# Gate and up products as a seven-product 2x2 block scheme, two tile pairs per part in native float32

## The chip, the cores and the metric
One core of one Trainium2 chip. The metric is the device time of one execution in microseconds; lower is better. Everything is float32 in memory. The kernel is written in Python over the engines' instructions: TensorE (PE) multiplies into PSUM, VectorE (DVE), ScalarE (ACT) and GpSimd (POOL) work element by element, SyncE (SP) issues the transfers.

## The reference, cut to what matters
Two layers of a streaming encoder for 592 tokens (16 learned ones, 512 of a prompt, 64 of a sample stream) with 1024 features. Each layer:

```python
h = h + 0.5 * swiglu(rms(h), wa_gate, wa_up, wa_down)      # 1024 -> 2816 -> 1024
h = h + mixer(rms(h))                                       # Mamba-2 and HGRN2 heads side by side
h = h + 0.5 * swiglu(rms(h), wb_gate, wb_up, wb_down)
# swiglu(x) = (silu(x @ w_gate) * (x @ w_up)) @ w_down
```

and a last RMS norm. So there are four SwiGLU parts (ffa and ffb of two layers); each has 22 pairs of gate and up tiles of 128 columns and 8 tiles of 128 output features. The states of the mixers are outputs too; the change doesn't touch them.

## The kernel before
Features lie on partitions, tokens along the rows, in two halves of 296 (288 in the last part, which leaves the learned tokens out). A product with weights is exact to float32 by splitting both sides into two float32r parts, high and low, and adding three products: high x high, high x low, low x high (lines 476, 477, 478; x first in the profile's names). The weights are split on chip after loading: the high part by ScalarE (line 430), the low part, raw minus high, by VectorE (line 437), 1024 elements per partition in one instruction each. The parts of the normed x (`nh`, `nl`) are made by `Norm.parts` (lines 578 to 582) from the residual `h` and the norm's weights; the factor 1/rms is applied after the product, in the sinks (`gate` line 647, `up` line 658), so a product needn't wait for it. `Norm.finish` computes it (sums of squares on TensorE, a power on GpSimd, spread to all partitions by TensorE, written by ScalarE at line 538).

The work is a list of `Job`s in the order of the weights: for each chunk of feature tiles (8, 7 and 7) gate and up tile by tile, then the eight `down` jobs of the chunk, whose sinks add to `h` (line 686). `products` walks this list on TensorE; `fetch` loads the raw weights in the same order (512 KB a load, three raw buffers, two of each split part).

What each engine does next is decided before the run by a planner. Every task is a Python generator that yields (engine, estimated ns, what it waits for, buffers needed) before each step; `Plan.run` always issues the step that can start first, with the lower rank among equals. A step may name two engines; the one that would end first gets it:

```python
t = yield (V, G), (ns_dve(n), ns_pool(n)), (t,), () if k0 else (blo,)
(V, G)[plan.pick].tensor_tensor(job.lo[:, k0:k1], job.raw[:, k0:k1], job.hi[:, k0:k1].bitcast(F32),
                                op=ALU.subtract)
```

The planner's costs are `ns_dve(n) = 68 + n / 0.96`, `ns_act(n) = 100 + n / 1.2`, `ns_pool(n) = 40 + 2.26 n`; it knows nothing of engines disturbing each other. Each engine then runs its own list in order, held only by semaphores. PSUM has four buffers for products with weights (`mm`) and four for all else (`aux`); 32 buffers of 592 columns (`bT`) serve everything in between.

Of the kernel before, what the change touches and what calls it, by code (L numbers as in the profile page):

```python
# [16 lines left out]
P = 128  # L17
# [27 lines left out]
def constants():  # L45
    """Constants of the shapes alone."""
# [60 lines left out]

def ns_dve(n):
# [76 lines left out]
def body(ctx: ExitStack, tc: tile.TileContext, a: dict, o: dict):  # L185
# [41 lines left out]
    # parameters with features on partitions, [128, layers * tiles of 128 features] each  # L227
# [39 lines left out]
    def load_scalars():  # L267
        # per-head scalars: dt_bias on 8 partitions; -exp(a_log) on all; d_skip by feature
# [21 lines left out]
        # lower bounds of the forget gates: clip(cumsum(softmax) - softmax[0], 0, 1 - 1e-6)  # L290
# [16 lines left out]
        # log(max(lb, 1e-30)) in two parts, each within Ln's range  # L307
# [70 lines left out]
    class Job:  # L378
# [3 lines left out]
        def __init__(self, name, src, ks, x, ev, hvs, sink, rank=1, few=0):  # L382
            self.rank, self.few = rank, few
            self.name, self.src, self.ks, self.x, self.ev, self.hvs, self.sink = name, src, ks, x, ev, hvs, sink
            self.ready = [Ev() for _ in ks]
# [3 lines left out]
    def fetch():  # L389
# [4 lines left out]
        for b in range(3):  # L394
            yield from fetch_x(b, 0)
            if b == 0:
                load_columns("a", [("ffa", 16, lt(a["ln_ffa_w"]))], -1)
        for i, job in enumerate(jobs):
            nk = len(job.ks)
            src = job.src.rearrange("(k p) c -> p k c", p=P)  # L400
            first = i == 0
            for k0, k1 in ((0, 4), (4, 8)) if first else ((0, nk),):
                t = yield "DMA", 190 * (k1 - k0), (), () if k0 else (braw,)
                if k0 == 0:
                    job.raw = braw.tile(f"wr{i}")
                SP.dma_start(job.raw[:, k0:k1, :src.shape[2]], src[:, k0:k1])
                split = Ev()
                plan.add(-1 if i < 2 else 0, convert(i, job, k0, k1, t + 2000.0, prev, split))
                prev = split
                if first:  # L410
                    for b, g in ((0, 1), (1, 1), (2, 1)) if k0 == 0 else ():
                        yield from fetch_x(b, g)
# [8 lines left out]
    def convert(i, job, k0, k1, t, prev, split):  # L421
        if job.few:
            yield from convert_few(i, job, t, prev, split)
            return
        n = (k1 - k0) * P
        t = yield (S, G), (ns_act(n), 700 + 0.95 * n), (t, prev) if prev else (t,), () if k0 else (bhi,)
        if k0 == 0:
            job.hi = bhi.tile(f"wh{i}")
        if plan.pick == 0:
            S.activation(job.hi[:, k0:k1], job.raw[:, k0:k1], AF.Copy)  # L430
        else:
            G.tensor_scalar(job.hi[:, k0:k1], job.raw[:, k0:k1], 1.0, 0.0, op0=ALU.mult, op1=ALU.add)
        split.set(0.0)
        t = yield (V, G), (ns_dve(n), ns_pool(n)), (t,), () if k0 else (blo,)
        if k0 == 0:
            job.lo = blo.tile(f"wl{i}")
        (V, G)[plan.pick].tensor_tensor(job.lo[:, k0:k1], job.raw[:, k0:k1], job.hi[:, k0:k1].bitcast(F32),  # L437
                                        op=ALU.subtract)
        if k1 == len(job.ks):
            braw.put(t)  # L440
        for r in job.ready[k0:k1]:
            r.set(t)

    def convert_few(i, job, t, prev, split):
        n = job.few
        t = yield S, ns_act(40 * KD), (t, prev), (bhi,)
        job.hi = bhi.tile(f"wh{i}")
        S.activation(job.hi[:, :, 0:40], job.raw[:, :, 0:40], AF.Copy)
        split.set(0.0)
        t = yield V, ns_dve(n * KD), (t,), (blo,)  # L450
        V.tensor_tensor(job.hi[:, :, 32:32 + n], job.raw[:, :, 0:n], job.hi[:, :, 0:n].bitcast(F32), op=ALU.subtract)
        braw.put(t)
        for r in job.ready:
            r.set(t)

    def products():
        # the first two jobs and the last two take turns, a half of the tokens each
        steps = [(job, hv) for job in jobs[2:-2] for hv in job.hvs]
        steps = [(job, hv) for hv in jobs[0].hvs for job in jobs[:2]] + steps
# [1193 lines left out]
```

## Time and profile before

| | |
|---|---|
| median of 3 runs | 2437.81 us (2435.04 to 2440.62) |
| span of the profiled execution | 2435.3 us (no separate device time is recorded for it) |
| TensorE busy | 2410.6 us, 99% |
| VectorE, ScalarE, GpSimd busy | 1329.0, 815.1, 148.8 us |
| moved by DMA | 188.16 MB, mean 77 GB/s |

A profile line of a group reads: source line, engine, operation, output <- inputs (partitions x elements), count, busy us and mean ns of one. Matmuls overlap in their pipeline, so a matmul's own duration (about 0.30 us) is longer than the distance from one start to the next; the distance, or pitch, is what counts for time. A line of the timeline reads: start, duration (of all xN together), engine, line, operation; in square brackets the idle time before it and what ended that.

### The profile page before, as it was taken

To read this page: it belongs to the slowest core of one execution; us is meant where nothing else is said; L and a number is where in the kernel's file an instruction comes from. 1 tells how busy PE (TensorE), PEld (TensorE's weight loads), DVE (VectorE), ACT (ScalarE), POOL (GpSimd) and SP (SyncE) were. 2 spreads that over 40 slices of the span, in tenths; PEclk is the share of its full clock that TensorE was granted. 3 is DMA by queue.
4 is the path that set the end of the run, shared out by engine and by line. 5 is a ranking of instruction groups with operands and counts; after the bars stand their busy time and mean duration, and the time that the engine had idled before them with its cause. 6 is when DMAs were issued, how large, how long until landed. Compare 5 with 4: busy or idle time off the path is not lost.

```text
span 2435.3 us, 42176 instructions
## 1 busy us (share of the span) xinstructions
PE 2410.6 (99%) x17919; PEld 2382.4 (98%) x17919; DVE 1329.0 (55%) x2431; ACT 815.1 (33%) x1450; POOL 148.8 (6%) x202
## 2 busy tenths in 40 slices
PE   8999999999999999999999999999999999999999
PEld 8999999999899999999999999999998999999998
DVE  6434345579957543444554343455799675444344
ACT  5212223346344321222333122233464543222232
POOL 2000000011301000000000000000122110000002
PEclk9999999999999999999999999999999999999999
DMA  5222222331112322222222222223311132322322
GB/s 152 78 79 83 82 79 78 81 85 42 28 49 74 92 78 82 82 81 79 78 87 79 79 86 80 78 79 87 79 42 37 48 96 79 87 82 78 92 76 78
DMA packets 363979, 188.16 MB, mean 77 GB/s; under 512 B 10384, under 2 KB 361408, under 8 KB 363792
## 3 DMA queue, kind: packets, MB, share of 16 engines
q1 hardware_dynamic: 363792, 185.47, 26.8%
q8 instruction: 141, 2.31, 0.4%
q14 instruction: 46, 0.38, 0.0%
HBM read 180.94 MB, written 4.51 MB: 76 GB/s over the span
## 4 chain that ended last, share of the span: by engine, by line
PE 95%; DVE 3%; POOL 1%; ACT 0%; issue 0%; DMA 0%; SPq 0%; DVEq 0%; ACTq 0%; POOLq 0%
PE pd L476 8%; PE pd L477 8%; PE pd L478 8%; PE pu L476 8%; PE pu L478 8%; PE pg L476 8%; PE pu L477 8%; PE pg L478 8%; PE pg L477 8%; PE px L478 1%; PE px L476 1%; PE px L477 1%; PE po L476 1%; PE po L478 1%; PE po L477 1%; PE pa L1024 1%
## 5 line engine op out<-in xcount | busy, mean ns | idle before, releaser
L430 ACT ACTIVATE wh<-wr 128x1024 fp32r<-128x1024 f32 (+2 forms) x361 | 361.2, 1001 | 838.1 <-PE pd L477 323.1
L437 DVE TENSOR_TENSOR wl<-wr,wh 128x1024 fp32r<-128x1024 f32 (+2 forms) x359 | 414.1, 1153 | 106.4 <-ACT wh L430 101.1
L476 PE MATMUL pd<-gh,wh 128*128 128x296 f32 (+3 forms) x1408 | 419.3, 298 | 0.0
L477 PE MATMUL pd<-gl,wh 128*128 128x296 f32 (+3 forms) x1408 | 418.7, 297 | 0.0
L478 PE MATMUL pd<-gh,wl 128*128 128x296 f32 (+3 forms) x1408 | 418.6, 297 | 0.0
L478 PEld LDWEIGHTS pd<-gh,wl 128*128 128x128 f32 x1408 | 265.1, 188 | 0.0
L476 PEld LDWEIGHTS pd<-gh,wh 128*128 128x128 f32 x1408 | 264.9, 188 | 0.0
L477 PEld LDWEIGHTS pd<-gl,wh 128*128 128x128 f32 x1408 | 264.9, 188 | 0.0
L686 DVE SCALAR_TENSOR_TENSOR h<-pd,h 128x296 f32<-128x296 f32 (+2 forms) x192 | 89.2, 464 | 264.5 <-PE pd L478 263.7
L476 PE MATMUL pg<-nh_a,wh 128*128 128x296 f32 x704 | 211.5, 300 | 0.0
L478 PE MATMUL pg<-nh_a,wl 128*128 128x296 f32 x704 | 211.1, 300 | 0.0
L476 PE MATMUL pu<-nh_a,wh 128*128 128x296 f32 x704 | 210.9, 300 | 0.0
L478 PE MATMUL pu<-nh_a,wl 128*128 128x296 f32 x704 | 210.7, 299 | 0.0
L477 PE MATMUL pg<-nl_a,wh 128*128 128x296 f32 x704 | 210.4, 299 | 0.0
L477 PE MATMUL pu<-nl_a,wh 128*128 128x296 f32 x704 | 210.1, 298 | 0.0
L476 PE MATMUL pg<-nh_b,wh 128*128 128x296 f32 (+1 forms) x704 | 209.7, 298 | 0.0
L476 PE MATMUL pu<-nh_b,wh 128*128 128x296 f32 (+1 forms) x704 | 209.5, 298 | 0.0
L477 PE MATMUL pg<-nl_b,wh 128*128 128x296 f32 (+1 forms) x704 | 209.2, 297 | 0.0
L477 PE MATMUL pu<-nl_b,wh 128*128 128x296 f32 (+1 forms) x704 | 209.0, 297 | 0.0
L478 PE MATMUL pu<-nh_b,wl 128*128 128x296 f32 (+1 forms) x704 | 208.9, 297 | 0.0
L478 PE MATMUL pg<-nh_b,wl 128*128 128x296 f32 (+1 forms) x704 | 208.9, 297 | 0.0
L670 ACT ACTIVATE gh<-ut 128x296 fp32r<-128x296 f32 (+1 forms) x176 | 79.2, 450 | 251.9 <-DVE ut L662 249.2
(404 smaller groups left out, 5250.5 us busy)
## 6 DMA issues: line engine op xcount, KB each, us to landing
wr<-in_w_in SPq DMA_DIRECT2D x56, 512.0 KB, 3.9
wr<-in_ffa_w_up SPq DMA_DIRECT2D x44, 512.0 KB, 3.8
wr<-in_ffb_w_gate SPq DMA_DIRECT2D x44, 512.0 KB, 3.9
wr<-in_ffb_w_up SPq DMA_DIRECT2D x44, 512.0 KB, 3.9
wr<-in_ffa_w_gate SPq DMA_DIRECT2D x43, 512.0 KB, 3.9
wr<-in_ffa_w_down SPq DMA_DIRECT2D x32, 448.0 KB, 3.8
wr<-in_ffb_w_down SPq DMA_DIRECT2D x32, 448.0 KB, 3.6
wr<-in_ffa_w_down SPq DMA_DIRECT2D x16, 512.0 KB, 4.2
```

Of the source, the lines that this page charges most:

```text
L430: S.activation(job.hi[:, k0:k1], job.raw[:, k0:k1], AF.Copy)
L437: (V, G)[plan.pick].tensor_tensor(job.lo[:, k0:k1], job.raw[:, k0:k1], job.hi[:, k0:k1].bitcast(F32), op=ALU.subtract)
L476: PE.matmul(out[:, :n], job.hi[:, j], xh, start=(j == 0), stop=False)
L477: PE.matmul(out[:, :n], job.hi[:, j], xl, start=False, stop=False)
L478: PE.matmul(out[:, :n], job.lo[:, j], xh, start=False, stop=(j == nk - 1))
L670: S.activation(g[0][:, sl], ut[:, :m], AF.Copy)
L686: V.scalar_tensor_tensor(h[:, m, sl], pt, 0.5, h[:, m, sl], op0=ALU.mult, op1=ALU.add)
L1024: PE.matmul(pt[:n, c0 // 2:(c0 + n) // 2], ks[:, c0:c0 + n], qs[:, c0 // 2:(c0 + n) // 2], start=True, stop=True)
```

## The change
Every pair of gate and up tiles except the first two of a part becomes a `Quad`. The product of x (two halves of tokens by two halves of features) with the weights (two halves of features by gate and up) has 2 x 2 x 2 block products of 512 features, 128 columns and 296 tokens; Strassen's scheme in Winograd's form needs seven, with sums of the weights and of x on the sides:

- The weights' sums (s1 = u1 + u2, s2 = s1 + g1, s4 = s2 + g2, s3 = g1 + u1, signs moved to the other side) are made by VectorE for each pair from the four raw loads, into the buffers `bzq`; then all seven weight blocks are split into float32r parts as before, 512 elements at a time.
- The sums of x are made once a part (`combinations`, `combine`): x is normed fully (the factor 1/rms included, so it is waited for), combined, and each of the 28 blocks is split into two parts held in `bT`.
- The seven products run one after the other on TensorE, adding up in three PSUM buffers; between them sinks copy or add sums out (`gated`), and four of the products wait for such a sink (`gates`).
- Pairs 0 and 1 of a part (`NPLAIN`) take the weights and the normed x as they are in native float32 (`whole`): no splits, one instruction for each product in the program.

With it come: loads, splits and buffers in units of four feature tiles (six raw, six high, six low); chunks of 6, 6, 5 and 5 tiles; the first `down` job of a chunk takes the last feature tile after both halves of the others (`late`); 50 instead of 32 `bT` buffers, which now also hold the mixers' `nh` and `nl`; other costs in the planner, and tasks of one part ranked by their place in the list; the last stores of the wide block by halves. Comments are gone too. Cut to the core:

```diff
-FF_CHUNKS = ((0, 8), (8, 15), (15, 22))
+FF_CHUNKS = ((0, 6), (6, 12), (12, 17), (17, 22))
+NPLAIN = 2
-NT = 32
+NT = 50
+UK = 4
 def ns_dve(n):
-    return 68 + n / 0.96
+    return 157 + n / 0.96
 def ns_act(n):
-    return 100 + n / 1.2
+    return 205 + n / 1.2
-    braw = Buf(sb, "raw", 3, [P, KD, P], F32)
-    bhi = Buf(sb, "whi", 2, [P, KD, P], F32R)
-    blo = Buf(sb, "wlo", 2, [P, KD, P], F32R)
+    braw = Buf(sb, "raw", 6, [P, UK, P], F32)
+    bhi = Buf(sb, "whi", 6, [P, UK, P], F32R)
+    blo = Buf(sb, "wlo", 6, [P, UK, P], F32R)
+    QUAD = (("g1", "b11", 0), ("s1", "t1", 1), ("s2", "t2", 0), ("s4", "b22", 1), ("s3", "t3", 0), ("g2", "b21", 2),
+            ("u2", "t4", 0))
...
+    def combine(i, got):
+        for name, p, q in (("s1", "u1", "u2"), ("s2", "s1", "g1"), ("s4", "s2", "g2"), ("s3", "g1", "u1")):
+            t = yield V, ns_dve(UK * P), (got[p][1], got[q][1]), (bzq,)
+            dst = got[name][0] = bzq.tile(f"ws{i}", [P, UK, P])
+            V.tensor_tensor(dst, got[p][0], got[q][0], op=ALU.add)
...
+    def convert(u, raw, chain, done, *waits):
...
+        t = yield (V, G), (ns_dve(n), ns_pool(n)), (t,), (blo,)
+        u.lo = blo.tile("wl")
+        (V, G)[plan.pick].tensor_tensor(u.lo[:, :u.n], raw, hi.bitcast(F32), op=ALU.subtract)
...
+                    if job.whole:
+                        PE.matmul(out[:, :n], u.hi[:, i], job.x(job.ks[j], sl), start=(j == 0), stop=(j == nk - 1))
+                        continue
...
+    def product_quad(job, i):
+        _, x, b = QUAD[i]
...
+        for j0 in range(0, UK, 2):
+            t = yield PE, ns_pass(n, 6), (u.ready, job.gates[i], *(job.ev(x, j) for j in (j0, j0 + 1))), \
+                (bmm,) if new and j0 == 0 else ()
...
+            for j in (j0, j0 + 1):
+                xh, xl = job.x(x, j)
+                PE.matmul(out, u.hi[:, j], xh, start=(new and j == 0), stop=False, skip_group_check=True)
+                PE.matmul(out, u.hi[:, j], xl, start=False, stop=False, skip_group_check=True)
+                PE.matmul(out, u.lo[:, j], xh, start=False, stop=(j == UK - 1), skip_group_check=True)
...
+        def combine(self, j, s0, after, begun):
...
+            t = yield V, 2 * ns_dve(w) + 120, (self.done, *((after,) if after else ())), (bT, bT, bT)
+            x1, x2, y = (bT.tile(f"{v}_{self.name}") for v in ("x1", "x2", "y"))
+            for x, k in ((x1, j), (x2, j + UK)):
+                V.scalar_tensor_tensor(x[:, :w], h[:, k, s0:T], weight(k), self.rstd[:, s0:T], op0=ALU.mult, op1=ALU.mult)
+            t = yield V, 3 * ns_dve(n) + 260, (t,)
+            V.tensor_tensor(y[:, lo], x2[:, hi], x1[:, hi], op=ALU.subtract)
+            V.tensor_tensor(x1[:, hi], x1[:, lo], x1[:, hi], op=ALU.subtract)
+            V.scalar_tensor_tensor(y[:, hi], x1[:, hi], -1.0, x2[:, hi], op0=ALU.mult, op1=ALU.subtract)
...
+    def gated(q, g, s0):
...
+            if i == 0:
+                t = yield S, ns_act(n), (t,), (bT,)
+                gg[0] = bT.tile("gg")
+                S.activation(gg[0][:, lo], acc, AF.Copy)
+                made.set(t)
+                q.gates[2].set(t)
+            elif i == 1:
...
+                S.activation(u2[0][:, :n], sec, AF.Copy)
+                q.gates[3].set(t)
+            elif i == 2:
...
+                S.activation(gg[0][:, hi], acc, AF.Copy)
+                q.gates[4].set(t)
+            elif i == 3:
...
+                V.tensor_tensor(gg[0][:, hi], sec, gg[0][:, hi], op=ALU.add)
...
+            elif i == 4:
...
+                V.scalar_tensor_tensor(u2[0][:, :n], acc, -1.0, u2[0][:, :n], op0=ALU.mult, op1=ALU.subtract)
+                q.gates[6].set(t)
+            elif i == 5:
...
+                V.tensor_tensor(gg[0][:, lo], third, gg[0][:, lo], op=ALU.add)
...
+                S.activation(gg[0][:, :2 * n], gg[0][:, :2 * n], AF.Silu)
+            else:
...
+                V.scalar_tensor_tensor(gg[0][:, lo], acc, -1.0, gg[0][:, lo], op0=ALU.mult, op1=ALU.mult)
...
+                V.tensor_tensor(gg[0][:, hi], u2[0][:, :n], gg[0][:, hi], op=ALU.mult)
...
+                S.activation(g[0][:, s0:], gg[0][:, :2 * n], AF.Copy)
...
+                V.tensor_tensor(g[1][:, s0:], gg[0][:, :2 * n], g[0][:, s0:].bitcast(F32), op=ALU.subtract)
...
-                jobs.append(Job(f"g{f}_", wg[:, fs], range(KD), norm.x, norm.x_ev, hvs, gate))
-                jobs.append(Job(f"u{f}_", wu[:, fs], range(KD), norm.x, norm.x_ev, hvs, up))
+                if f < NPLAIN:
+                    jobs.append(Job(f"g{f}_", wg[:, fs], range(KD), norm.x, norm.x_ev, hvs, gate, whole=True))
+                    jobs.append(Job(f"u{f}_", wu[:, fs], range(KD), norm.x, norm.x_ev, hvs, up,
+                                    after=norm.put if f == NPLAIN - 1 else None, whole=True))
+                    continue
+                jobs.append(Quad(f"q{f}_", wg[:, fs], wu[:, fs], norm.qx, norm.qx_ev, norm.n, None,
+                                 norm.qput if f == NFF - 1 else None))
+                jobs[-1].sink = gated(jobs[-1], gs[f - c0], s0)
```

## Rows read from the trace of the kernel before
**Rows 1.** The page: busy time by engine, and shares of the chain.
```profile
PE 2410.6 (99%) x17919; PEld 2382.4 (98%) x17919; DVE 1329.0 (55%) x2431; ACT 815.1 (33%) x1450; POOL 148.8 (6%) x202
PE 95%; DVE 3%; POOL 1%; ACT 0%; issue 0%; DMA 0%; SPq 0%; DVEq 0%; ACTq 0%; POOLq 0%
```
**Rows 2.** Windows: stretch, length, busy by engine (x instructions), clock, DMA share, GB/s.
```profile
797.00:1190.00 393.00, 392.96 (x2883) 392.71 (x2882) 173.82 (x283) 104.13 (x157) 2.87 (x3) 1.00 0.28 81
447.50:797.00 349.50, 342.05 (x2551) 327.65 (x2550) 260.43 (x540) 156.88 (x330) 56.24 (x72) 0.98 0.22 59
550.00:700.00 150.00, 142.55 (x1078) 130.14 (x1076) 127.42 (x283) 76.35 (x172) 35.02 (x25) 0.95 0.15 40
```
**Rows 3.** Windows of the gate product's matmuls alone (296, then 288 columns).
```profile
250.00:300.00 50.00, 6.71 (x48) 1.00 0.27 81
2250.00:2300.00 50.00, 6.53 (x48) 1.00 0.30 85
```
**Rows 4.** Timeline of TensorE: native float32 products of 192 columns in a mixer.
```profile
654.24 0.82 PE L1085 MATMUL pd<-qd,kk 128*128 128x192 f32 x4
654.89 0.30 PE L1088 MATMUL pd<-q,kk 128*80 128x80 f32 x2
...
655.14 0.90 PE L1085 MATMUL pd<-qd,kk 128*128 128x192 f32 x4
655.74 0.43 PE L476 MATMUL pgg<-nh_m,wh 128*128 128x296 f32 x1
```
**Rows 5.** Groups of VectorE by form: the low part of 512 weights.
```profile
L437 DVE TENSOR_TENSOR wl<-wr,wh 128x512 fp32r<-128x512 f32 x32 | 22.0, 686 | 3.3 <-ACT wh L430 2.0
```
**Rows 6.** Timeline of VectorE: independent operations in a mixer; a dependent pair.
```profile
619.24 0.67 DVE L1300 TENSOR_TENSOR xdt<-xT,dtt 128x512 f32<-128x512 f32 x1
619.84 0.67 DVE L1302 TENSOR_TENSOR xw<-xT,wst 128x512 f32<-128x512 f32 x1
620.44 0.40 DVE L1308 TENSOR_TENSOR cbm<-bT,cf 128x256 f32<-128x256 f32 x1
620.77 0.45 DVE L993 TENSOR_TENSOR qs<-ks,q 128x296 f32<-128x296 f32 x1
621.14 0.68 DVE L1355 TENSOR_TENSOR ss<-ss,etot 128x512 f32<-128x512 f32 x1
...
117.78 0.47 DVE L658 TENSOR_TENSOR ut<-pu,rs_a 128x296 f32<-128x296 f32 x1 [1.03 <-PE pu L478]
118.28 0.47 DVE L662 TENSOR_TENSOR ut<-ut,gt 128x296 f32<-128x296 f32 x1
```
**Rows 7.** Groups of ScalarE by form: the high part of 512 weights; a copy of 296.
```profile
L430 ACT ACTIVATE wh<-wr 128x512 fp32r<-128x512 f32 x34 | 21.4, 631 | 40.8 <-PE po L477 26.8 <-PE pz L477 7.8 <-issue 4.0
L670 ACT ACTIVATE gh<-ut 128x296 fp32r<-128x296 f32 x132 | 59.6, 452 | 190.8 <-DVE ut L662 188.4
```
**Rows 8.** First gate products of a part; timeline of ScalarE: 1/rms written.
```profile
L476 PE MATMUL pg<-nh_b,wh x7: 298/299/302, 797.3 to 799.8; 128*128 128x296 f32 x7
807.36 0.42 ACT L538 ACTIVATE rs_b<-ra_b 128x296 f32<-128x296 f32 x1 [0.92 <-PE ra_b L534]
808.46 0.42 ACT L538 ACTIVATE rs_b<-ra_b 128x296 f32<-128x296 f32 x1 [0.68 <-PE ra_b L534]
```
**Rows 9.** Timeline of SP: one weight load issued. DMA issues: 256 KB, us to landing.
```profile
1004.72 0.37 SPq L406 DMA_DIRECT2D wr<-in_ffb_w_up  x1
wr<-in_w_out SPq DMA_DIRECT2D x32, 256.0 KB, 2.7
```
**Rows 10.** Timeline: GpSimd beside VectorE in a mixer; group of GpSimd's weight splits.
```profile
612.49 1.03 POOL L1319 TENSOR_TENSOR ls<-cf,lah 128x512 fp32r<-128x512 f32 x1
...
615.48 1.03 POOL L1319 TENSOR_TENSOR ls<-cf,lal 128x512 fp32r<-128x512 f32 x1
...
614.02 3.18 DVE L993 TENSOR_TENSOR qs<-ks,q 128x288 f32<-128x288 f32 x2 [2.90 <-ACT ks L767]
L437 POOL TENSOR_TENSOR wl<-wr,wh 128x512 fp32r<-128x512 f32 x2 | 3.3, 1659 | 13.4 <-ACT wh L430 13.4
```

More of the change, by code (lines that the diff above doesn't have):

```diff
@@ L397, in fetch @@
                 load_columns("a", [("ffa", 16, lt(a["ln_ffa_w"]))], -1)
+        chain = [None]
         for i, job in enumerate(jobs):
-            nk = len(job.ks)
+            if isinstance(job, Quad):
+                yield from fetch_quad(i, job, chain)
+                continue
             src = job.src.rearrange("(k p) c -> p k c", p=P)
[L401 to L410, printed above, removed]
+            for k0, k1, u in job.units:
+                t = yield "DMA", 190 * (k1 - k0), (), (braw,)
+                raw = braw.tile(f"wr{i}", [P, k1 - k0, src.shape[2]])
+                SP.dma_start(raw, src[:, k0:k1])
+                t += 2000.0
+                if job.whole:
+                    u.hi = raw
+                    u.ready.set(t)
+                elif job.few:
+                    plan.add(near(job.order), convert_few(i, job, u, raw, t, chain))
+                else:
+                    plan.add(near(job.order), convert(u, raw, chain, braw.put, t))
+                if i == 0:
                     for b, g in ((0, 1), (1, 1), (2, 1)) if k0 == 0 else ():
@@ L419, in fetch, with fetch_quad @@
                 load_params()
[L421 to L428, printed above, removed]
+    def fetch_quad(i, job, chain):
+        half = UK * P
+        got = {}
+        for name, w, r0 in (("g1", job.wg, 0), ("u1", job.wu, 0), ("u2", job.wu, half), ("g2", job.wg, half)):
+            t = yield "DMA", 190 * UK, (), (braw,)
+            raw = braw.tile(f"wr{i}")
+            SP.dma_start(raw, w[r0:r0 + half].rearrange("(k p) c -> p k c", p=P))
+            got[name] = [raw, Ev(), Ev({"g1": 3}.get(name, 2), braw.put)]
+            got[name][1].set(t + 2000.0)
+        for name, n in (("s1", 2), ("s2", 2), ("s4", 1), ("s3", 1)):
+            got[name] = [None, Ev(), Ev(n, bzq.put)]
+        plan.add(near(job.order), combine(i, got))
+        for k, ((name, _, _), u) in enumerate(zip(QUAD, job.units)):
+            raw, ev, use = got[name]
+            plan.add(near(job.order + k), convert(u, got[name], chain, use.set, ev))
@@ new lines, in combine @@
+    def combine(i, got):
[3 more added lines that the diff above has]
+            V.tensor_tensor(dst, got[p][0], got[q][0], op=ALU.add)
+            got[name][1].set(t)
+            got[p][2].set(t)
+            got[q][2].set(t)
+    def convert(u, raw, chain, done, *waits):
+        prev, chain[0] = chain[0], Ev()
+        split = chain[0]
+        n = u.n * P
+        t = yield (S, G), (ns_act(n), 700 + 0.95 * n), (*waits, prev) if prev else waits, (bhi,)
+        if isinstance(raw, list):
+            raw = raw[0]
+        u.hi = bhi.tile("wh")
+        hi = u.hi[:, :u.n]
@@ new lines, in products @@
+                    PE.matmul(out[:, :n], u.hi[:, i], xl, start=False, stop=False)
+                    PE.matmul(out[:, :n], u.lo[:, i], xh, start=False, stop=(j == nk - 1))
+            if ks.stop < nk:
+                continue
+            plan.add(job.rank if job.rank >= SHARED else near(job.order + 2), job.sink(hf, sl, out[:, :n], t))
+            if hf == job.hvs[-1][0]:
+                if job.whole:
+                    braw.put(t, len(job.units))
+                else:
+                    bhi.put(t, len(job.units))
+                    blo.put(t, len(job.units))
+                if job.after:
+                    job.after(t)
@@ new lines, in products @@
+        last_product.set(t)
+    def product_quad(job, i):
+        _, x, b = QUAD[i]
+        u, n = job.units[i], job.n
+        new = job.sums[b] is None
+        more = b == 0 and i < 6 or i == 1
+        for j0 in range(0, UK, 2):
+            t = yield PE, ns_pass(n, 6), (u.ready, job.gates[i], *(job.ev(x, j) for j in (j0, j0 + 1))), \
+                (bmm,) if new and j0 == 0 else ()
+            if new and j0 == 0:
+                job.sums[b] = bmm.tile(f"p{job.name}{b}")
+            out = job.sums[b][:, :n]
+            for j in (j0, j0 + 1):
[3 more added lines that the diff above has]
+                PE.matmul(out, u.lo[:, j], xh, start=False, stop=(j == UK - 1), skip_group_check=True)
+        plan.add(near(job.order + i + 2), job.sink(i, [s if s is None else s[:, :n] for s in job.sums], t))
+        bhi.put(t)
+        blo.put(t)
+        if i == 6 and job.after:
+            job.after(t)
@@ L584, in parts, with combinations @@
+            if not self.whole:
+                t = yield V, ns_dve(n) + 60, (t,)
+                V.scalar_tensor_tensor(self.lo[m][:, sl], h[:, m, sl], w, hi.bitcast(F32), op0=ALU.mult, op1=ALU.subtract)
             self.ev[m][hf].set(t)
+        def combinations(self, s0):
+            self.n = (T - s0) // 2
+            self.q = {}
+            self.q_ev = [[Ev() for _ in range(UK)] for _ in range(4)]
+            self.pair4 = [[None, Ev()], [None, Ev()]]
+            begun = None
+            for j in range(UK):
+                begun, b = Ev(), begun
+                plan.add(near(self.order + 2 * NPLAIN - 1), self.combine(j, s0, b, begun))
@@ L634, in ffn @@
     def ffn(norm, wg, wu, wd, nxt, hvs, tail=None):
+        s0 = hvs[0][1].start
+        norm.order = places[0]
+        norm.combinations(s0)
         for c0, c1 in FF_CHUNKS:
@@ L695, in ge @@
                         return gs[k][2][2 if i else hf]
[L696 removed]
+                    jobs.append(Job(f"d{m}_", wd[c0 * P:c1 * P, m * P:(m + 1) * P], range(n), gx, ge, dhv, down, late=m == 0 and dhv is hvs))
     att = []
```

255 lines of the change are left out of this document (176 added, 79 removed).

## Prediction
> **What bounds the kernel now.** First the page's busy shares and chain [rows 1]: TensorE is busy 99% of the span and carries 95% of the chain that ended last, VectorE 55%, ScalarE 33%, GpSimd 6%. A busy TensorE alone proves little, so next the windows [rows 2]: in one SwiGLU part (797 to 1190 us) 2883 matmuls stand in 392.96 busy us of 393.00, 0.1363 us each, without a gap, beside a VectorE busy 174 us. A mixer's windows show TensorE idle 7.4 us of 349.5, all of it where VectorE is 85% busy (550 to 700). So in the SwiGLU parts time is the number of matmuls times their pitch, and VectorE has half its time free there. From the windows restricted to the gate product [rows 3]: 48 matmuls of 296 columns take 6.71 us; without the last one's 0.16 us that outlasts the pitch this is 0.1365 us each. With 288 columns: 0.1327.
>
> The profiled span is 2435.3 us, the median 2437.8. The profile shows no separate time for that execution, so I sum against the span and add 2.5 us at the end. A measurement can tell about 0.2% (4.9 us) from no change.
>
> **Removed.** A pair of gate and up tiles takes 8 block products of 4 x 3 matmuls per half of the tokens; a Quad takes 7. That is 12 matmuls less, for 20 pairs in each of four parts: 60 x 12 x 0.1365 = 98.3 and 20 x 12 x 0.1327 = 31.8. Together -130.1 us, all on the path.
>
> **Added on TensorE.** Pairs 0 and 1 of each part run in native float32: 64 products instead of 64 triples. The trace records a native product as two matmuls: four records of 192 columns take 654.24 to 654.89, 0.1625 us each [rows 4]; scaled to 296 columns 0.2505, so 0.501 a product against 3 x 0.1365 = 0.4095. That is +5.9 us a part, 23.3 for four (the last has 288 columns). Ends: the next four records stand in 0.60 us [rows 4], which gives +14; four passes (the planner's figure for float32) at the float32r pitch would give +35. TensorE's net: -106.8.
>
> **VectorE in a Quad.** New are 4 sums of raw weights and 7 splits of 512 elements (before, 2 splits of 1024). A lone 512-element split takes 0.686 us [rows 5], but independent operations follow each other at 0.60 for 512 elements and 0.37 for 296 [rows 6]. The sinks are five operations of 296 elements, one pair dependent at 0.50 [rows 6], and one of 592 (0.68 on the same line). 11 x 0.60 + 4 x 0.40 + 0.50 + 0.68 = 9.4 us against TensorE's 84 x 0.1365 = 11.47; by lone durations about 10.7. It fits, at 82 to 93%. ScalarE's 7 copies of 512 at 0.631 and sinks of 0.45 to 0.7 [rows 7] make about 7.2. Both are hidden by TensorE; that cover shrinks from half of the time to a tenth.
>
> Inside a Quad four products wait for a sink of an earlier one, with one product (1.64 us) between. A sink on ScalarE costs 0.2 + 0.45 + 0.1 and up to 0.63 behind a conversion, in time. The one on VectorE (gate of the last product) costs 0.77 and up to 0.69 behind a split: 1.46, just in time. What is queued ahead there decides; I take 0.1 us a Quad, 8 us (0 to 48).
>
> **Start of each part.** The plain pairs cover 64 x 0.50 = 32 us. The combinations of x wait for the root mean square: the part starts at 797.3 and the second half of it is written at 808.46 + 0.42 [rows 8], 11.6 us later. VectorE then owes, for each of four feature tiles, two operations of 592 (0.75 as scalar_tensor_tensor), three of 296 (1.3), three splits of 592 (2.05) and 0.85 for the last: 5.0, together 20; the plain tiles' sinks 7; the first Quad's weights 6.6. Up to the first Quad's product: 4 x 2.8 first steps, 5.5 of sinks, 2.8 of splits, four sums 2.4, two weight splits 1.2: 23.1, so 34.7 against 32. Of the remaining 15 us, TensorE's six products cover 9.8. A stall of 2.7 + 5.2 = 7.9 us if VectorE does all of it in that order; next to nothing if GpSimd takes splits without a price. I take 5.5, 22 us for four parts (0 to 36).
>
> **Ends of chunks.** The output projection now starts after the last Quad's last product, and its g passes two VectorE steps, a copy of 592 and a subtraction: about 3.2 us, up to 4.7 with something ahead. The two first halves without the last feature tile cover 4.1 us (chunks of 6) or 3.3 (of 5). 16 ends at 0.6: 10 us (0 to 22). The last chunk has no such cover on its second half: +2.
>
> **Costed at nothing.** Four chunks instead of three: 16 more additions to h a part on VectorE, beside 33 to 39 us of matmuls. Twice as many weight loads of half the size: about 750 issues at 0.37 us [rows 9] is 280 us of SP's 2370; each lands in 2.7 us [rows 9], six buffers ahead of an 11.5 us Quad. Mixer weights in two pieces: 44 x 0.05 us of VectorE a layer, mostly outside its busy 150 us; with the planner's new costs reordering that stretch, -6 to +12 in all. The last stores: two more issues on SP, at most 0.7.
>
> **Sum.** -130.1 + 23.3 + 8 + 22 + 10 + 2 = -64.8; span 2370.5, median 2373.
>
> **A rule against this.** Where four GpSimd products run from 612.49 to 616.5, two VectorE products that take 0.37 each elsewhere take 3.18 us together [rows 10]. The planner lets GpSimd take a weight split when VectorE is late, and prices it at 1.2 us with no cost to VectorE; two such splits took 1.659 us each [rows 10]. The Trainium skill, "SBUF — State Buffer", section "Who interferes with whom", says why: a VectorE operation with two SBUF inputs and a GpSimd one that reads SBUF exclude each other for a whole instruction. The trace agrees, as far as that one stretch goes. What it would make of the time is the third rival.
>
> **Rivals.**
> 1. Only TensorE counts: order and buffers hide all stalls but some 8 us. 2435.3 - 106.8 + 8 + 2.5 = 2339. For it: VectorE's 174 of 393 us, and no gap in the parts now. Against: the 11.6 us before the combinations can begin. Chance 0.18.
> 2. The gates inside a Quad: VectorE's sink arrives late by half a microsecond or more, each time. 80 x 0.5 more: 2413. Against: 1.46 us fits 1.64. Chance 0.13.
> 3. Slower: GpSimd's splits lock VectorE. Place: every Quad. With 3 of 7 splits on GpSimd at 1.66 us, VectorE standing still meanwhile: 8 x 0.60 + 2.9 + 5.0 = 12.7 us against 11.47, 80 x 1.2 = 98 more: 2471. It decides from 12.3 us a Quad on, where 80 x 0.8 eats the 64.8. For it: the 3.18 us. Against: VectorE's own work leaves 2 us a Quad, so the planner needs GpSimd seldom. Chance 0.10.
> 4. The change does not do what it says: native float32 at more than four passes' price, or TensorE waiting for weights as long as it saves: 2438. The records of native products speak against it. Chance 0.02.
>
> **How the numbers follow.** My forecast, TensorE-bound Quads with short stalls at the starts and chunk ends, has 0.57; its own range is 2348 to 2400. Faster: 0.57 + 0.18 + 0.13 = 0.88; same 0.02; slower 0.10. The range of 2336 to 2425 holds the first rival and the second up to a late sink of 0.65 us a Quad, and leaves out the third and the low end of the first.
>
> **What the profile after must show.** 84 matmul records to a Quad at the same 0.1365 us; native records of 0.25 us, 128 in each part; in the SwiGLU windows TensorE busy to 96 to 98% with its gaps at the first Quad of each part, waiting for the split parts of x; VectorE at 80 to 93% in Quads; GpSimd with at most two weight splits a Quad. I am wrong if TensorE waits in every Quad (rivals 2 and 3: for the negated sum, or for wl from GpSimd), if pitches grow, or if the mixers' 350 us move by more than 8.

## The result, and the profile after

The kernel after takes 2411.4 us in the median (2410.12 to 2411.77, 4 runs), the kernel before in the same runs 2438.2 (2435.04 to 2440.62): a ratio of 0.9891, 95% interval 0.9877 to 0.9905. That is faster by 27 us (1.1%), where 65 were forecast. The profiled execution's span fell from 2435.3 to 2409.7 us.

The page of the kernel after, busy time by engine and shares of the chain that ended last, against [rows 1]:

```profile
PE 2333.8 (97%) x16703; PEld 2262.8 (94%) x16703; DVE 1747.8 (73%) x3130; ACT 980.6 (41%) x1987; POOL 627.7 (26%) x630
PE 38%; DVE 5%; issue 2%; DMA 1%; POOL 1%; ACT 0%; DVEq 0%; ACTq 0%; POOLq 0%
```

The shares of this chain add up to 47% only: it could not be followed back through the whole span, so its 38% can't be held against the 95% of [rows 1]. TensorE is no longer without gaps, and the engine that grew most is the one whose work the forecast took as free: GpSimd, from 148.8 to 627.7 us. Its groups in the kernel after, weight splits (L524), VectorE's sums of weights beside them (L502), and two operations of the sinks (L891, L881); the columns are those of [rows 5]:

```profile
L524 POOL TENSOR_TENSOR wl<-wr,wh 128x512 fp32r<-128x512 f32 x105 | 157.4, 1502 | 147.1 <-ACT wh L518 133.6 <-DVE ws L502 9.3
L502 DVE TENSOR_TENSOR ws<-wr,wr 128x512 f32<-128x512 f32 x160 | 142.1, 888 | 59.4 <-DMA wr<-in_ffa_w_up 35.4 <-DMA wr<-in_ffb_w_up 22.6 <-POOL wl L524 1.2
L524 POOL TENSOR_TENSOR wl<-ws,wh 128x512 fp32r<-128x512 f32 x87 | 135.3, 1560 | 266.5 <-ACT wh L518 242.4 <-DVE ws L502 12.2 <-DVE gg L872 4.1
L502 DVE TENSOR_TENSOR ws<-ws,wr 128x512 f32<-128x512 f32 x160 | 134.2, 839 | 1.3 <-POOL wl L524 0.8
...
L891 DVE TENSOR_TENSOR gg<-u,gg 128x296 f32<-128x296 f32 x60 | 44.0, 733 | 0.0
L881 DVE TENSOR_TENSOR gg<-pq,gg 128x296 f32<-128x296 f32 x60 | 27.6, 460 | 12.1 <-PE pq L609 12.1
```

With two smaller groups of 16 (narrower splits of other stages) GpSimd makes 224 low parts of weights; before, it made two [rows 10]. A sum of 512 elements on VectorE takes 839 to 888 ns in the mean, where a lone operation of that size took 686 [rows 5]. Not every operation of VectorE grew: the product L891, with both inputs in SBUF, takes 733 ns in the mean, but the sum L881, as long and with one input in PSUM (`pq`), 460.

Windows of the kernel after: from 829.6 us the first four Quads of part b0, from 886.5 its first chunk of `down` products, from 925.7 the next six Quads, and below these the two mixers (the columns are those of [rows 2]):

```profile
829.60:886.50 56.90, 49.02 (x337) 47.70 (x337) 49.81 (x70) 24.91 (x49) 23.36 (x17) 0.94 0.30 88
886.50:925.70 39.20, 39.20 (x291) 39.20 (x290) 19.68 (x38) 8.36 (x15) 4.00 (x4) 1.00 0.29 85
925.70:997.10 71.40, 69.76 (x507) 68.89 (x506) 53.12 (x82) 34.61 (x66) 22.74 (x18) 1.00 0.30 87
...
446.80:795.90 349.10, 338.64 (x2550) 326.21 (x2549) 266.24 (x538) 142.21 (x328) 109.47 (x119) 0.99 0.22 58
1641.80:1986.40 344.60, 336.33 (x2550) 323.61 (x2550) 268.33 (x541) 142.75 (x329) 104.29 (x120) 0.99 0.22 59
```

The 336 matmuls of the first four Quads would fill 45.9 us at the old pitch of 0.1365 and take 56.9; the 504 of six later Quads would fill 68.8 and take 71.4; the `down` chunk of 288 fills its 39.2 us. GpSimd's busy time in the first mixer doubled, from 56.24 [rows 2] to 109.47 us.

Where the time went, by stages read from the first and last records of each stage's products in the two traces (us; the last column is the first experiment's kernel, below):

| term | forecast | after | splits off GpSimd |
|---|---|---|---|
| 12 matmuls less a Quad, 80 Quads | -130.1 | as counted, pitch unchanged | as counted |
| first two pairs in native float32 | +23.3 | +23.4 | +23.4 |
| starts: first four Quads of each part, beyond their matmuls | +22 | +55.9 | +31.5 |
| gates: later Quads, beyond their matmuls | +8 (all Quads) | +17.5 | +2.7 |
| chunk ends | +10 | 0 | 0 |
| last chunk | +2 | +0.9 | +1.2 |
| both mixers together (684.7 before) | 0 | +9.0 | -17.1 |
| span | -64.8 | -25.6 | -90.8 |

The two measured columns miss their spans by some 2 us, because a stage's last record outlasts the start of the next by 0.2 us. The starts hold two things. By the distances between the matmuls' starts, some 44 of the 55.9 us are waits, and some 11 are matmuls behind these waits at a lower clock (105 of them, 0.245 us apart instead of 0.1365; see experiment 8); of the 31.5 us in the last column some 24 and 6.

What TensorE waited for, in the kernel after (the view of waits: engine, tile and line, waited for; us in all, times, longest):

```profile
PE pq L608 <- DVE ql_a L794: 12.3, 8, 3.9
PE pq L608 <- DVE ql_b L794: 12.2, 7, 4.2
PE pq L607 <- DVE u L877: 11.1, 24, 1.3
PE oT L1443 <- ACT yt L1436: 7.5, 2, 5.4
...
PE pq L607 <- ACT u L864: 5.6, 9, 3.3
PE pS L1623 <- DVE xw L1581: 4.9, 2, 2.5
...
PE pq L609 <- POOL wl L524: 1.9, 1, 1.9
```

`ql` are the low parts of x's combinations, at the starts of parts; `u` is the copy or negated sum of the gates; `yt` and `xw` are in the mixers. For a low part from GpSimd itself (the last line) TensorE waited only once, 1.9 us: it isn't the slowness of GpSimd's own splits that it meets. The start of part b0 shows how this comes about. Timelines of GpSimd, VectorE and TensorE in the kernel after:

```profile
829.06 2.56 POOL L524 TENSOR_TENSOR wl<-ws,wh 128x512 fp32r<-128x512 f32 x1 [12.04 <-ACT wh L518]
831.60 1.14 POOL L520 TENSOR_SCALAR wh<-wr 128x512 fp32r<-128x512 f32 x1
832.71 2.73 POOL L524 TENSOR_TENSOR wl<-ws,wh 128x512 fp32r<-128x512 f32 x2
835.39 5.01 POOL L524 TENSOR_TENSOR wl<-wr,wh 128x512 fp32r<-128x512 f32 x3
```

```profile
834.23 1.52 DVE L934 TENSOR_TENSOR ut<-ut,gt 128x296 f32<-128x296 f32 x1
835.68 3.59 DVE L794 TENSOR_TENSOR ql_b<-y_b,qh_b 128x592 fp32r<-128x592 f32 x2
839.19 1.53 DVE L944 TENSOR_TENSOR gl<-ut,gh 128x296 fp32r<-128x296 f32 x1
840.65 0.76 DVE L794 TENSOR_TENSOR ql_b<-y_b,qh_b 128x592 fp32r<-128x592 f32 x1
841.34 3.95 DVE L794 TENSOR_TENSOR ql_b<-x_b,qh_b 128x592 fp32r<-128x592 f32 x7
```

```profile
833.12 0.29 PE L607 MATMUL pq<-qh_b,wh 128*128 128x296 f32 x1
837.57 0.41 PE L608 MATMUL pq<-ql_b,wh 128*128 128x296 f32 x1 [4.16 <-DVE ql_b L794]
```

While GpSimd makes six weight splits from 829.06 to 840.4, a VectorE product of 296 elements (at 834.23) lasts 1.52 us instead of 0.4 to 0.5 [rows 6], and two splits of 592 (at 835.68) last 1.8 each instead of 0.76. (Not every operation in that time is hit: a product of 296 at 830.02 took 0.46.) From 841.34, with GpSimd done, seven of them follow each other in 3.95 us, 0.56 each. GpSimd's own split takes 1.3 to 2.6 us meanwhile. It is the pattern of [rows 10], now at the place where TensorE waits. The Trainium skill, "SBUF — State Buffer", section "Who interferes with whom", says that a VectorE operation with two SBUF inputs and a GpSimd operation that reads SBUF exclude each other for a whole instruction. The trace of after agrees: the product of 834.23 ends at 835.75, 0.31 us after the pair of splits that GpSimd ended at 835.44, and L881, with one input in SBUF, didn't grow.

### The profile page after: what moved, and what is told of

Its sections match the earlier page's. It is cut to its first block, busy times and chain, and to the rows that moved or that the text cites. A ratio compares the mean times of both kernels' runs of the same rounds, so it can differ in the third digit from the quotient of the medians.

```text
span 2409.7 us, 43335 instructions
## 1 busy us (share of the span) xinstructions
PE 2333.8 (97%) x16703; PEld 2262.8 (94%) x16703; DVE 1747.8 (73%) x3130; ACT 980.6 (41%) x1987; POOL 627.7 (26%) x630
## 5 line engine op out<-in xcount | busy, mean ns | idle before, releaser
L518 ACT ACTIVATE wh<-wr 128x512 fp32r<-128x512 f32 (+2 forms) x461 | 263.0, 571 | 371.3 <-PE pd L579 236.7
L524 DVE TENSOR_TENSOR wl<-wr,wh 128x512 fp32r<-128x512 f32 (+2 forms) x503 | 336.3, 686 | 45.2 <-ACT wh L518 42.0
L607 PE MATMUL pq<-qh_a,wh 128*128 128x296 f32 x1120 | 341.0, 304 | 10.8 <-DVE u L877 6.0
L608 PE MATMUL pq<-ql_a,wh 128*128 128x296 f32 x1120 | 339.0, 303 | 12.3 <-DVE ql_a L794 12.3
L608 PE MATMUL pq<-ql_b,wh 128*128 128x296 f32 (+1 forms) x1120 | 336.2, 300 | 12.2 <-DVE ql_b L794 12.2
L607 PE MATMUL pq<-qh_b,wh 128*128 128x296 f32 (+1 forms) x1120 | 335.8, 300 | 6.1 <-DVE u L877 5.1
L609 PE MATMUL pq<-qh_a,wl 128*128 128x296 f32 x1120 | 338.0, 302 | 1.9 <-POOL wl L524 1.9
L609 PE MATMUL pq<-qh_b,wl 128*128 128x296 f32 (+1 forms) x1120 | 335.2, 299 | 0.0
L524 POOL TENSOR_TENSOR wl<-wr,wh 128x512 fp32r<-128x512 f32 (+2 forms) x137 | 197.5, 1444 | 400.9 <-ACT wh L518 386.1
L607 PEld LDWEIGHTS pq<-qh_a,wh 128*128 128x128 f32 x1120 | 214.0, 191 | 16.5 <-issue 7.8
L608 PEld LDWEIGHTS pq<-ql_a,wh 128*128 128x128 f32 x1120 | 214.1, 191 | 14.9 <-DVE ql_a L794 14.8
```

The lines of the kernel that those rows point to most:

```text
L518: S.activation(hi, raw, AF.Copy)
L524: (V, G)[plan.pick].tensor_tensor(u.lo[:, :u.n], raw, hi.bitcast(F32), op=ALU.subtract)
L607: PE.matmul(out, u.hi[:, j], xh, start=(new and j == 0), stop=False, skip_group_check=True)
L608: PE.matmul(out, u.hi[:, j], xl, start=False, stop=False, skip_group_check=True)
L609: PE.matmul(out, u.lo[:, j], xh, start=False, stop=(j == UK - 1), skip_group_check=True)
```

## The experiments

The first theory, LOCK, says that the low parts on GpSimd hold VectorE up and TensorE waits for that. Its rival, LOAD, says that VectorE has too much to do and needs GpSimd's help. Of a ratio, "to before" means the kernel before on the same chip.

**1. All low parts on VectorE** (from the kernel after):

```diff
-        t = yield (V, G), (ns_dve(n), ns_pool(n)), (t,), (blo,)
+        t = yield (V,), (ns_dve(n),), (t,), (blo,)
```

> The changed kernel with all 224 low-part splits that GpSimd had moved to VectorE. Theory LOCK (a split on GpSimd stops VectorE's operations with two SBUF inputs for about its own length, so handing splits to GpSimd delays the split parts of x at the start of a part, the sinks in the Quads and the mixers): the stall of a part's first four Quads falls from 11 to 20 us to about 8 (VectorE's own work), the later Quads' 17 us to about 5, the second mixer loses its 9 us: 2367 us, 2355 to 2385. Theory LOAD (VectorE has too much to do at the start of a part, and GpSimd's help is help): 8 splits more for VectorE at each start, 0.6 us each, 5 us a part: 2431 us, 2415 to 2445.

Measured: 2346.36 us (2345.69 to 2347.18), 0.9625 to before, interval 0.961 to 0.9639. The page, windows of the first four Quads of b0, the six later ones and the mixers, VectorE's sums of weights by form, and TensorE's waits, in this kernel:

```profile
PE 2308.9 (98%) x16703; PEld 2247.7 (96%) x16703; DVE 1725.1 (74%) x3354; ACT 980.4 (42%) x1970; POOL 319.0 (14%) x423
```

```profile
801.50:854.50 53.00, 48.75 (x339) 48.12 (x338) 45.53 (x82) 22.66 (x44) 6.10 (x7) 0.94 0.33 94
...
893.70:962.50 68.80, 68.80 (x506) 68.80 (x505) 55.45 (x94) 35.33 (x66) 5.41 (x6) 1.00 0.31 91
433.10:768.00 334.90, 334.53 (x2551) 322.83 (x2550) 257.84 (x555) 143.28 (x329) 75.94 (x99) 1.00 0.23 61
1595.10:1928.00 332.90, 331.46 (x2550) 319.66 (x2550) 255.83 (x555) 143.02 (x329) 75.80 (x104) 1.00 0.23 61
```

```profile
L502 DVE TENSOR_TENSOR ws<-wr,wr 128x512 f32<-128x512 f32 x160 | 123.0, 769 | 25.0 <-DMA wr<-in_ffa_w_up 14.6 <-DMA wr<-in_ffb_w_up 9.9
L502 DVE TENSOR_TENSOR ws<-ws,wr 128x512 f32<-128x512 f32 x160 | 109.2, 683 | 0.3
```

```profile
PE pq L609 <- DVE wl L524: 15.6, 6, 4.5
...
PE pq L608 <- DVE ql_a L794: 2.1, 4, 0.8
PE pq L607 <- DVE u L877: 2.0, 2, 1.7
```

One line of the program gives 65 us, more than LOCK's range of 2355 to 2385 had. VectorE runs 224 instructions more (3354 against 3130) and is busy 22.7 us less: GpSimd's help cost VectorE more than the helped work. The product L891 takes 459 ns in the mean again, where L881 stays at 465. The wait for the negated sum fell from 24 times to 2, so the late gates too were GpSimd's doing. LOCK holds, and was priced too low, in the mixers above all (9 us expected, 26 found); LOAD falls. What stays at the starts is a wait for `wl` from VectorE.

**2. High parts off GpSimd as well**, the 226 high parts that GpSimd makes in experiment 1 (one SBUF input, a scaled copy) on ScalarE alone:

```diff
-        t = yield (S, G), (ns_act(n), 700 + 0.95 * n), (*waits, prev) if prev else waits, (bhi,)
+        t = yield (S,), (ns_act(n),), (*waits, prev) if prev else waits, (bhi,)
...
-        t = yield (V, G), (ns_dve(n), ns_pool(n)), (t,), (blo,)
+        t = yield (V,), (ns_dve(n),), (t,), (blo,)
```

> As the run before, and the 206 high-part copies of weights that GpSimd had moved to ScalarE too. LOCK: these copies read SBUF as well and hold VectorE, so a few us less than with the low parts alone: 2362 us, 2350 to 2380. LOAD: ScalarE has 60% of its time free, so the same as with the low parts alone, 2431 us, 2415 to 2445.

Measured: 2348.94 us (2346.66 to 2350.14), 0.9635 to before (0.9619 to 0.9651): no faster than experiment 1. Its page:

```profile
PE 2309.4 (98%) x16703; PEld 2248.8 (96%) x16703; DVE 1701.1 (73%) x3354; ACT 1092.4 (47%) x2190; POOL 141.4 (6%) x203
```

VectorE's busy time falls by 24 us once more, so these copies hold it up a little too (its 160 sums of raw weights take 686 ns in the mean, where they took 769 in experiment 1), but the time doesn't follow. That they stand where VectorE has slack would explain it, and isn't shown. LOCK's range of 2350 to 2380 was too high for the reason that it was in experiment 1, the price of the low parts; the few us that it gave these copies did not show.

**3 and 4. Where the 65 us lie.** Low parts on VectorE in Quads only (74 others stay on GpSimd), then only in the first two Quads of each part (188 stay):

```diff
-            plan.add(near(job.order + k), convert(u, got[name], chain, use.set, ev))
+            plan.add(near(job.order + k), convert(u, got[name], chain, use.set, ev, lone=True))
...
-        t = yield (V, G), (ns_dve(n), ns_pool(n)), (t,), (blo,)
+        t = yield ((V,), (ns_dve(n),), (t,), (blo,)) if lone else ((V, G), (ns_dve(n), ns_pool(n)), (t,), (blo,))
```

(in the second `lone=job.name in ("q2_", "q3_")`)

> Low-part splits of the Quads' weights on VectorE alone; those of the mixers and of the down tiles as in the changed kernel (74 on GpSimd are left). LOCK: the starts and the Quads gain as in the first run, the mixers don't: 8 us above it, 2375 us, 2360 to 2390. LOAD: as the first run, 2431 us.

> Low-part splits of the first two Quads of each part on VectorE alone, all others as in the changed kernel. LOCK: only the starts gain, 24 us: 2387 us, 2378 to 2400. LOAD: only the starts lose, 20 us: 2431 us.

Measured: 2372.79 us (2369.89 to 2373.68), 0.9731 to before (0.9717 to 0.9746), and 2394.52 us (2391.5 to 2396.98), 0.9822 (0.9807 to 0.9836). So of the 65 us the first two Quads of each part hold 17, the other Quads 22, and the rest, the mixers above all, 26. LOCK had 24 us for the starts and 8 for the mixers. Read by stages, the two mixers take 695 us in the first of these kernels (GpSimd busy 110 us in its first mixer) and 668 without GpSimd's splits. Each of these edits also lets the planner order the other steps anew, which these times hold too.

**5. More cover, less cover.** Two theories for the 7.9 us of stall that are left at each start. LOAD-FIRST: VectorE owes too much before the first Quad, and time spent in native pairs covers it. ORDER: it is the sequence in which VectorE takes its steps, which more cover would not change. One native pair instead of two, and three:

```diff
-NPLAIN = 2
+NPLAIN = 1
```

```diff
-NPLAIN = 2
+NPLAIN = 3
...
-            yield "none", 0, (e4, ends[1], ends[2])
-            bT.put(max(e4.t, ends[1].t, ends[2].t), 3)
+            yield "none", 0, (ends[1], ends[2])
+            bT.put(max(t, ends[1].t, ends[2].t), 2)
+            yield "none", 0, (e4,)
+            bT.put(e4.t)
```

(both with all low parts on VectorE; the second also gives scratch buffers back sooner, so that 50 are enough)

> Low parts on VectorE alone, one plain pair a part instead of two. TensorE saves 4 x (1.64 + 2.9) = 18 us, the cover of VectorE's work at a start shrinks by 16 us, its own work by 3.5. LOAD-FIRST: 2346 - 18 + 4 x 12.5 = 2378 us, 2365 to 2390. ORDER: the stall stays, 2328 us.

> Low parts on VectorE alone, three plain pairs a part, scratch buffers freed sooner. TensorE pays 18 us more, the cover grows by 16 us a part. LOAD-FIRST: the 32 us of stalls at the starts go: 2346 + 18 - 30 = 2334 us, 2326 to 2345. ORDER: 2364 us.

Measured: 2375.05 us (2374.53 to 2375.17), 0.9749 to before (0.9734 to 0.9763), and 2336.86 us (2336.72 to 2337.22), 0.9593 (0.9578 to 0.9607). LOAD-FIRST holds in both directions. A third native pair costs 4 x (16.0 - 11.5) = 18 us, from 64 records of 0.25 us against a Quad's 84 of 0.1365, and the kernel is 9.5 faster, so it gives 27.5 back.

**6. The first Quad's weights earlier.** Its raw loads right behind the part's first native tile, so that its sums and splits are made before 1/rms is there (low parts on VectorE, two native pairs; for want of buffers the run also gives scratch buffers back sooner, and the copies of x's fourth combination wait until the native x is done with):

```diff
+        firsts = [i for i, job in enumerate(jobs) if isinstance(job, Quad) and job.name == f"q{NPLAIN}_"]
+        for i in firsts:
+            loads.insert(2 if i == 2 * NPLAIN else i - 2 * NPLAIN + 1, loads.pop(i))
```

> The kernel with low parts on VectorE alone, and the raw weights of a part's first Quad loaded right behind the part's first plain tile (second in the first part) instead of behind all four; two scratch buffers of the x combinations freed sooner so that the buffers suffice. Theory LOAD-FIRST (what is left of the stall at a start, 7.9 us a part, is VectorE's own work, and the first Quad's sums and splits, 6.6 us of it, can move into the 11 us before 1/rms is known): 2346 - 4 x 6 = 2322 us, 2312 to 2335. Rival ORDER (the wait is for the x parts and their chain, not for the amount of VectorE's work): within 5 us of 2346.

Measured: 2341.36 us (2341.06 to 2342.3), 0.9611 to before (0.9597 to 0.9626): 5 us better than experiment 1, where 24 were expected. The time is outside LOAD-FIRST's range and just inside ORDER's, but it is a sum of two things. By stages the three later parts gained 5.2, 4.1 and 4.1 us, and TensorE's waits in their first four Quads fell from 5.1, 5.4 and 4.0 us to 0.2, 1.5 and 0.2, as LOAD-FIRST has it; the first part lost 7.7. TensorE's longest wait in this kernel, and SyncE's issue of the gate weights of the first part's second native pair, here and in experiment 1:

```profile
PE pg L575 <- DVE y_a L772: 7.4, 1, 7.4
```

```profile
31.54 3.54 SPq L466 DMA_DIRECT2D wr<-in_ffa_w_gate  x2
```

```profile
14.65 1.07 SPq L462 DMA_DIRECT2D wr<-in_ffa_w_gate  x2
```

The first part's native stage stops before its second pair, until 39.33 us, and took 48.5 us instead of 37.8. The view names a step of x's combinations (`y_a`), which ended just then, but a native product reads no combination: its weights were asked for 17 us later than in experiment 1, behind those of the first Quad. At the start of the program the order of loads that helps the other parts hurts.

**7. Both, each where it helps.** Three native pairs and the old order of loads in the first part, two pairs and the early loads in the other three:

```diff
-            loads.insert(2 if i == 2 * NPLAIN else i - 2 * NPLAIN + 1, loads.pop(i))
+            loads.insert(i - 2 * NPLAIN + 1, loads.pop(i))
...
+        norm.np = np = NPLAIN + (norm.name == "a0")
```

> Low parts on VectorE only; the first part with three native pairs and its loads in the old order, the other three parts with two native pairs and the first Quad's raw weights loaded right behind the first plain tile. PLACES (the early loads do shorten the start of a part, by 5.2, 4.1 and 4.1 us in b0, a1 and b1 as read from the trace of the run with early loads; there the first part lost 7.7 us, because at the start of the program TensorE still waits for transfers and the early load stands in front of the plain tiles' own): 2346.4 - 13.4 - 3.1 (three native pairs in the first part) = 2330, between 2326 and 2336, TensorE's granted clock above 0.99. Rival SHIFT (a start that is shortened in one place gives the time back in the following chunk or mixer): no faster than the run with three native pairs everywhere, 2337 or more.

Measured: 2332.55 us (2330.72 to 2332.66), 0.9574 to before (0.9558 to 0.959). It lies in PLACES' range, and this is the fastest kernel of the study, 79 us below the kernel after. From three native pairs everywhere it is 4 us, between two chips, and the intervals of the two ratios overlap, so the stages have to speak against SHIFT: the first four Quads of the three later parts take 47.8, 49.1 and 46.4 us here and 53.2, 52.7 and 50.6 in experiment 1, and the first part is 4 us shorter too. Of these 17 us 14 reach the end. TensorE's two longest waits:

```profile
PE xT L353 <- DMA x<-in_x_prompt: 6.6, 3, 4.6
PE pq L611 <- DVE u L885: 2.9, 5, 1.6
```

**8. Is it the clock?** Behind the long waits of the kernel after, TensorE's granted clock fell. Its windows at the start of b0, the clock being the third column from the end, and two matmuls there:

```profile
834.00:837.00 3.00, 0.00 (x0) 0.00 (x0) 3.00 (x3) 1.53 (x4) 3.00 (x3) 1.00 0.06 17
837.00:840.00 3.00, 1.34 (x6) 1.11 (x6) 3.00 (x3) 0.00 (x0) 3.00 (x2) 0.68 0.34 95
840.00:843.00 3.00, 1.97 (x8) 1.60 (x8) 3.00 (x5) 0.42 (x1) 0.41 (x1) 0.50 0.27 79
```

```profile
842.62 0.45 PE L609 MATMUL pq<-qh_b,wl 128*128 128x296 f32 x1
842.87 0.45 PE L607 MATMUL pq<-qh_b,wh 128*128 128x296 f32 x1
```

Behind the wait of 4.16 us at 833.4 it went to 0.50, the lower of its two levels (1.2 instead of 2.4 GHz), and matmuls start some 0.245 us apart instead of 0.1365. To see whether that costs time, 30 matmuls whose sum nothing uses were put in front of the third product of each part's first Quad (kernel after otherwise):

```diff
+        if i == 2 and job.name == f"q{NPLAIN}_":
+            u0 = job.units[1]
+            t = yield PE, ns_pass(n, 30), (), (baux,)
+            junk = baux.tile("junk")[:, :n]
+            for j in range(30):
+                PE.matmul(junk, u0.hi[:, j % UK], job.x("t1", j % UK)[0], start=True, stop=True)
+            baux.put(t)
```

> The changed kernel with 30 idle matmuls (4.1 us) on TensorE ahead of the third product of each part's first Quad, where it waits for the split parts of x. If that wait is as long as it looks, they cost nothing, and if TensorE's granted clock falls because of the gap and costs time afterwards, they win some: 2411 - 8 = 2403 us, 2395 to 2409 with a clock above 0.986. If the clock is without effect on the time: 2411, 2408 to 2414. If TensorE is not waiting there: 2427.

Measured: 2411.01 us (2406.2 to 2416.64), 0.989 to before (0.9868 to 0.9912). The timeline of TensorE in this kernel, at b0:

```profile
835.02 4.23 PE L604 MATMUL junk<-qh_b,wh 128*128 128x296 f32 x30
839.09 0.30 PE L614 MATMUL pq<-qh_b,wh 128*128 128x296 f32 x1
...
843.84 0.50 PE L615 MATMUL pq<-ql_b,wh 128*128 128x296 f32 x1 [1.46 <-DVE ql_b L801]
844.14 0.45 PE L616 MATMUL pq<-qh_b,wl 128*128 128x296 f32 x1
```

Sixteen us of extra matmuls, four at each start, cost nothing: TensorE really was waiting there. Nor did they gain anything that these runs can tell. But they don't settle what the clock costs, since they didn't keep it up: they only moved its fall behind a later wait (0.45 us in the records from 844.14 on), and in the first four Quads of the parts 97 matmuls followed each other at the slower distance, where it had been 105. What the slower matmuls can cost stands in the traces: some 11 us at the starts of the kernel after and 6 in experiment 1; how much of that waiting for VectorE would have taken anyway is open. With three native pairs (experiment 5) and in experiment 7, where the waits are short, the clock is 1.00 from 16 us to some 3 us before the end.

**9. Why the planner turned to GpSimd.** The kernel before with nothing but the new prices of VectorE and ScalarE:

```diff
-    return 68 + n / 0.96
+    return 157 + n / 0.96
...
-    return 100 + n / 1.2
+    return 205 + n / 1.2
```

> The kernel before with nothing but the planner's new prices for VectorE and ScalarE. UNITS (GpSimd gets the low parts because the change halves their size, so that GpSimd's price is only 507 ns above VectorE's instead of 1219 ns before): still only a handful of low parts on GpSimd, time within 5 us of before, 2433 to 2443. Rival PRICES (the dearer VectorE alone sends the splits to GpSimd): dozens of low parts of 1024 on GpSimd at about 3.3 us each, mixers longer by 10 us or more each, 2455 or more.

Measured: 2449.87 us (2448.62 to 2451.67), 1.0058 to before (1.0043 to 1.0073). GpSimd's group of weight splits in this kernel, by form:

```profile
L437 POOL TENSOR_TENSOR wl<-wr,wh 128x512 fp32r<-128x512 f32 x2 | 3.3, 1658 | 13.4 <-ACT wh L430 13.4
```

Still two low parts, so the prices alone don't send them to GpSimd; that much of UNITS holds. Its time does not: the kernel is 14 us slower, neither UNITS' 5 nor PRICES' 20. The second mixer takes 346.9 us instead of 335.4, the first 344.2 instead of 349.3: another order of nearly the same work (GpSimd has 8 instructions more, five of them high parts of 1024) moves a mixer by 5 to 11 us. That the half-size units are the cause is argued, not shown: they were not tried alone, and VectorE's added work and the tasks' new ranks came with them.

## Why the prediction was wrong

**What held.** The sign, and the measured time lies in the stated range of 2336 to 2425 us, though above the forecast's own of 2348 to 2400; the forecast was too fast by 38 us. The matmuls saved and their pitch are as counted. The native pairs cost +23.4 us against 23.3 forecast. TensorE is the bound, and its gaps stand where the text put them, at the first Quad of each part behind the split parts of x. One of the text's own signs of being wrong showed: the second mixer grew from 335.4 to 344.6 us, by more than 8.

**The step that failed** is the one on who makes the weights' low parts. In "Start of each part" the sum said 7.9 us of stall "if VectorE does all of it in that order; next to nothing if GpSimd takes splits without a price", and took 5.5. The first number was met: with every low part on VectorE the starts lose 31.5 us, 7.9 a part. That it was met so closely is luck. By the paragraph's own prices a feature tile of x owes 5.7 us and not 5.0 (two operations of 592 at 0.75, not one), and beyond the 23.1 us up to the first Quad's product 4 x 5.7 + 7 + 6.6 - 23.1 = 13.3 us remain, not 15, which gives a stall of 2.7 + 3.5 = 6.2; and of the measured 7.9 some 6.0 are waits, 9.4 in the first part and 4.0 to 5.4 in the others, and 1.6 are matmuls at the lower clock, which no term had. The second number had the wrong sign. GpSimd's splits have a price, it falls on VectorE, and the starts took 55.9 us, 14 a part. Of the 39 us by which the span was missed, 33.9 are this term, and 24.4 of them went with GpSimd's splits. The row with that price, 3.18 us for two products [rows 10], stood in the prediction, and was used only for a rival.

The same omission runs through two more terms. The gates were priced by queueing on VectorE alone, at 8 us, and cost 17.5; without GpSimd's splits later Quads cost 2.7, so that the working of a sink "just in time" was sound. The mixers were costed at nothing, on VectorE's 44 x 0.05 us, and grew by 9.0 us; there the planner hands 35 low parts of 512 elements to GpSimd, where it handed two before, beside VectorE's own busiest stretch. Only the chunk ends came out cheaper, 0 instead of 10 us. The chunks' `down` windows hold no gap.

**Rival 3** had the mechanism and the wrong place and price. In the middle Quads of a chunk GpSimd does take three of the seven low parts, as it assumed; over all 80 Quads it makes 150 (224 less the 74 of the other stages), fewer than two a Quad. The timelines of GpSimd and of VectorE in one such Quad of the kernel after:

```profile
949.97 1.29 POOL L524 TENSOR_TENSOR wl<-wr,wh 128x512 fp32r<-128x512 f32 x1 [0.55 <-DVE ws L502]
```

```profile
950.26 1.54 DVE L502 TENSOR_TENSOR ws<-wr,wr 128x512 f32<-128x512 f32 x1
```

A sum of 0.68 us becomes 1.54, but that is 0.9 us lost and not GpSimd's whole 1.66, and VectorE has slack in a Quad: six Quads lost 71.4 - 68.8 = 2.6 us, 0.4 each where 1.2 was priced. The lock decides at the starts, where VectorE has none; in the mixers too by experiment 3, though there a new order of the work came with it. The argument against it, that "the planner needs GpSimd seldom", was not worked out. With splits of 512 the planner's price for GpSimd is 40 + 2.26 x 512 = 1197 ns against 157 + 512 / 0.96 = 690 for VectorE, so that it chooses GpSimd as soon as VectorE's queue is 0.5 us long; with 1024 the gap was 2354 - 1135 = 1219. The prices stood in the text on the kernel before and in the diff.

**Rivals 1 and 2.** The 2339 us of rival 1, TensorE alone, are out of reach of the kernel after, but not of the scheme: three native pairs pass them with 2337, experiment 7 with 2333. That the measured 2411 is close to rival 2's 2413 is chance: its late gates are there, but cost 17.5 us and not 40, and are a part of the lock: 24 waits for the negated sum in the kernel after, 2 in experiment 1.

**Open.** Without GpSimd's splits the mixers take 17.1 us less than before the change, although their matmuls are the same. TensorE's waits in them sum to 11.8 us before, 18.7 in the kernel after and 1.8 without GpSimd's splits, so some 10 of the 17 are waits that went. Experiment 9 shows that order moves them by some ten too; what of the 17 is order, finer units or GpSimd's absence was not separated. Nor was it tried how the first part could have its first Quad's weights early without losing 7.7 us.

## What to carry to other kernels

A second engine that "helps" is priced by what it does to the first one, not by its own duration: look for the row where both run at once, and put its price into every term where a planner may choose that engine. When a change halves the size of a unit, work out again at what backlog the planner's choice flips. And a bound that moves from one engine to order and latency asks for cover in front of the first dependent product: here a costlier native pair paid for itself one and a half times.

## What the runs showed of the hardware that was not expected

VectorE was busy 22.7 us less with 224 more instructions, once GpSimd no longer made splits of two inputs beside it. Of its steps in the Quads' sinks those with two SBUF inputs were longer beside GpSimd (a product of 296: 733 ns in the mean, 459 without the splits); one of the same size with an input in PSUM took 460 and 465. GpSimd's scaled copies with one SBUF input, 226 in experiment 1 and none in experiment 2, lengthened VectorE's busy time by 24 us, and the whole by nothing that the runs can tell. And 30 idle matmuls in a wait of 4 us did not keep TensorE's granted clock up through the waits behind it.
